# First transfers reordered and split, and twelve products of zeros ahead of the first real one, in a one-core encoder layer

## The chip, the cores and the metric

The kernel runs on one core of one Trainium2 chip. The core has a matrix engine (PE, with its own weight loads, PEld), a vector engine (DVE), a scalar engine (ACT), GpSimd (POOL), a queue engine (SP) that here starts the transfers, and 16 DMA engines that the queues share. The metric is the device time of one execution in microseconds (us); lower is better. It is given as the median of several runs.

## The reference: what is computed

One layer of an encoder trunk on x of 1 x 2048 x 1024 in float32. Cut to what matters here:

```python
xn = rms_norm(x, mix_norm_g)                 # mean of squares over 1024 features, then a gain
proj = xn @ w_in                             # w_in: 1024 x 5640
aq, ak, av, mq, mk, mv, mo, i, f, ga, gm = split(proj)
A = chunk_band_attention(aq, ak, av, rel_bias)     # 8 heads, own chunk of 64 and 8 before it
M = mlstm_chunkwise(conv(mq), conv(mk), mv, i, f)  # 4 heads, matrix memory
y = sigmoid(ga) * (A @ w_att_proj) + sigmoid(gm) * (M @ w_mlstm_proj)
x = x + y @ w_out
x = x + relu(rms_norm(x) @ w_up) ** 2 @ w_down
out = rms_norm(x)
```

The first thing that the matrix engine computes is `av`, the attention values of the first 512 tokens.

## The kernel before, in words

The 2048 tokens are worked in four blocks of 512. A float32 product is made of three products of a rounded form (fp32r): a value is split into a high part (a copy rounded to fp32r, on ACT) and a low part (the value less its high part, on DVE), and `mm3` (L642) multiplies high by high, high by low and low by high into one PSUM bank (lines 644, 645 and 646). Later parts of the program use seven instead of eight products of quarter matrices (`quad`, line 727).

Weights come as tiles of 128 x 1024 float32 (512 KB). `loader` (L509) starts their transfers into four raw tiles, `wraw`; `split_w` (L563) starts the transfer and `split_now` (L579) makes the two parts into one of three `wsp` tiles: ACT's copy is line 583, DVE's subtraction line 585. The first four weight tiles make `av` for the first block. Each of them covers two depth tiles of 128 features and 512 columns.

Block 0 is not normalised before its first products. `norm_in` and `square_in` (L1171) load x, transposed, as eight depth tiles of 128 x 512 (256 KB, line 1178), multiply each with its gain on ACT into the high part (line 1182), make the low part on DVE (line 1184), square it on ACT (line 1192) and add up the squares on DVE (line 1196); the rows are scaled by the root when a bank is emptied. The gains are in `gcol`, 12 KB, whose transfer is the second on SP (`setup`, line 430). Transfers of x and of the first four weight tiles take turns by events (`x_sent`, `w_sent`).

`token_tiles` (L666) multiplies: per weight tile, four token tiles `t` (one PSUM bank each), and in each two depth tiles `k`, three products each; 24 products for a weight tile, 96 for `av`. x is the stationary operand there, the weights move.

Two planners set the order. `Flow` runs the program's parts as threads with estimated times and gives out buffers and banks. `Order` then takes all instructions, their dependences and estimated durations, and writes a fixed order for each engine. PE's order goes by the thread's order among what is ready, the others' by due times. So the order on an engine is fixed before the run, and an instruction waits for the one ahead of it on its engine and for its operands.

Of the kernel before, what the change touches and what calls it, by code (L numbers as in the profile page):

```python
# [24 lines left out]
F32 = mybir.dt.float32  # L25
# [5 lines left out]
P = 128  # L31
# [4 lines left out]
NT = T // P  # L36
# [59 lines left out]
class Flow:  # L96
# [7 lines left out]
               act=dict(pe=220.0, act=130.0, dve=130.0, pool=180.0),  # L104
               dve=dict(pe=220.0, act=130.0, dve=130.0, pool=155.0), pool=dict(pe=290.0, act=130.0, dve=60.0),
               sp=dict())
# [106 lines left out]
def act_ns(n, ps=False, ap=0):  # L213
    return (51 if ps else 93) + 0.834 * n + 93 * ap


def dve_ns(n):
    return 70 + 1.042 * n
# [154 lines left out]
class Layer:  # L373
# [50 lines left out]

    def setup(self):
        nc, io = self.nc, self.io
        nc.vector.memset(self.half, -0.5)
        nc.vector.memset(self.ones, 1.0)
        yield "sp", 50
        nc.sync.dma_start(self.gcol, io["gcol"].rearrange("p (a b) -> p a b", a=3))  # L430
        self.fl.set(self.ev_gain)
        yield "wait", [self.w_sent[2]]
        yield "sp", 700, 2000
        nc.sync.dma_start(self.const, io["consts"].rearrange("p (a b) -> p a b", a=2))
        self.fl.set(self.ev_const)
# [73 lines left out]
    def loader(self):  # L509
        fl, io = self.fl, self.io  # L510
        i = 0
        for kind, n in self.weights():
            if kind == "quad":
                raws, evs = [], [Event() for _ in range(4)]
                fl.spawn(self.quad_w(i, *n, raws, evs), 0)
                for j in range(4):
                    (raw,) = yield "get", self.wraw, 1
                    raws.append(raw)
                    fl.spawn(self.load_w(io["wf"][n[0], j], raw, evs[j]), 0)
                i += 7  # L520
                continue
            first = kind == "plain" and i < KT // 2
            if kind == "plain":
                src = io["w"][n]
            else:
                q, m = n
                given, x = ((0, 0), (0, 2), (1, 0), (1, 1), (0, 3), (1, 2), (1, 3))[m]
                if given and q in self.td_ev:
                    yield "wait", self.td_ev[q]
                src = (io["wf"][q], self.td[q].ap() if given else None)[given][x]  # L530
            (raw,) = yield "get", self.wraw, 1
            if first:
                yield "wait", [self.x_sent[2 * i]]
            fl.spawn(self.split_w(i, src, raw, self.w_sent[i] if first else None), 0)
            i += 1

    def sum_w(self, q):
# [25 lines left out]
    def split_w(self, i, src, raw, sent=None):  # L563
        yield "sp", 1750, 2000
        self.nc.sync.dma_start(raw, src)
        if sent is not None:
            self.fl.set(sent)
        yield from self.split_now(i, raw)
        self.fl.put(self.wraw, raw, late=self.LATE)

    def slot_w(self, i):

        if i > 0:
            yield "wait", [self.wgot[i - 1]]
        (w,) = yield "get", self.wsplit, 1
        self.fl.set(self.wgot[i])
        return w
# [88 lines left out]
    def token_tiles(self, srcs, evs, after):  # L666

        fl = self.fl
        bank = [None] * NT
        nw = len(srcs) // 2  # L670
        for i in range(nw):
            w = yield from self.next_w()
            wv = w.rearrange("p a (k c) -> p a k c", k=2)
            for t in range(NT):
                if i == 0:
                    (bank[t],) = yield "dense", self.banks, 1
                for k in range(2):
                    g = 2 * i + k
                    if evs[g] is not None:
                        yield "wait", [evs[g]]  # L680
                    yield "pe", 681
                    a = srcs[g][:, :, t * P:(t + 1) * P]
                    self.mm3(bank[t], a[:, 0], a[:, 1], wv[:, 0, k], wv[:, 1, k],
                             g == 0, g == 2 * nw - 1)
                if i == nw - 1:
                    fl.spawn(after(t, bank[t]), 1)
            fl.put(self.wsplit, w, late=self.LATE_SPLIT)

# [1900 lines left out]
```

## Time and profile before

| | us |
|---|---|
| median of 3 runs | 2778.67 |
| lowest and highest of them | 2775.3 and 2782.26 |
| span of the profiled execution (first to last instruction) | 2771.8 |
| PE busy in it | 2749.0 |
| first product starts at | 6.37 |

For the profiled execution only its span is given, with no time of its own beside it; the median of the runs lies 6.87 us above that span. PE is busy for 99% of the span. "Busy" counts a product from its start to its end, and products overlap: one of 512 columns lasts about 0.39 us, and the next starts about 0.227 us after it. The distance between starts is therefore the rate. Times in the views are from the first instruction on. A transfer has a time of issue on its queue and, later, one of landing.

### The profile page before, as it was taken

To read this page: it belongs to the slowest core of one execution; us is meant where nothing else is said; L and a number is where in the kernel's file an instruction comes from. 1 tells how busy PE (TensorE), PEld (TensorE's weight loads), DVE (VectorE), ACT (ScalarE), POOL (GpSimd) and SP (SyncE) were. 2 spreads that over 40 slices of the span, in tenths; PEclk is the share of its full clock that TensorE was granted. 3 is DMA by queue.
4 is the path that set the end of the run, shared out by engine and by line. 5 is a ranking of instruction groups with operands and counts; after the bars stand their busy time and mean duration, and the time that the engine had idled before them with its cause. 6 is when DMAs were issued, how large, how long until landed. Compare 5 with 4: busy or idle time off the path is not lost.

```text
span 2771.8 us, 38590 instructions
## 1 busy us (share of the span) xinstructions
PE 2749.0 (99%) x12994; PEld 2285.1 (82%) x12994; DVE 2056.7 (74%) x3783; ACT 1491.5 (54%) x2608; POOL 54.7 (2%) x100
## 2 busy tenths in 40 slices
PE   9999999999999999999999999999999999999998
PEld 7888888888778888888888888888888888888887
DVE  7796789768996866886676688889888656555565
ACT  5564576535454535575555566666335655554443
POOL 0010001000000000000000000000000000000000
PEclk9999999999999999999999999999999999999999
DMA  7968759768765677589877977877977667766574
GB/s 275 294 193 276 230 166 306 248 224 318 258 205 203 220 252 255 194 273 326 289 280 273 296 236 233 257 228 234 290 247 254 209 220 262 242 239 218 190 229 151
DMA packets 329046, 678.64 MB, mean 245 GB/s; under 512 B 36840, under 2 KB 67728, under 8 KB 328848
## 3 DMA queue, kind: packets, MB, share of 16 engines
q1 hardware_dynamic: 328848, 676.18, 73.0%
q8 instruction: 102, 1.67, 0.3%
q14 instruction: 96, 0.79, 0.1%
HBM read 472.59 MB, written 203.44 MB: 244 GB/s over the span
## 4 chain that ended last, share of the span: by engine, by line
PE 94%; DMA 2%; DVE 2%; issue 2%; ACT 0%; SPq 0%; POOLq 0%; POOL 0%; DVEq 0%; ACTq 0%
PE bank L727 44%; PE bank L644 12%; PE bank L645 12%; PE bank L646 12%; PE bank L1417 2%; PE bank L1390 2%; PE bank L1448 2%; PE bank L755 2%; PE bank L1702 1%; PE bank L1703 1%; PE bank L1704 1%; PE bank L1688 0%; DVE wsp L585 0%; DMA r<-u 0%; DMA r<-kfar 0%
## 5 line engine op out<-in xcount | busy, mean ns | idle before, releaser
L727 PE MATMUL bank<-r,wsp 128*128 128x512 f32 x5544 | 1265.6, 390 | 0.9 <-DVE ctx L2083 0.4
L727 PEld LDWEIGHTS bank<-r,wsp 128*128 128x128 f32 x5544 | 1037.9, 188 | 222.3 <-DVE ctx L1869 3.7
L585 DVE TENSOR_TENSOR wsp<-wraw,wsp 128x1024 fp32r<-128x1024 f32 x459 | 561.2, 1223 | 357.6 <-ACT wsp L583 353.3
L583 ACT CAST wsp<-wraw 128x1024 fp32r<-128x1024 f32 x459 | 482.3, 1051 | 506.0 <-PE bank L727 210.6
L644 PE MATMUL bank<-r,wsp 128*128 128x512 f32 x1472 | 586.4, 399 | 1.8 <-ACT r L1226 1.6
L645 PE MATMUL bank<-r,wsp 128*128 128x512 f32 x1472 | 575.2, 391 | 0.2 <-DVE r L1231 0.2
L646 PE MATMUL bank<-r,wsp 128*128 128x512 f32 x1472 | 575.2, 391 | 0.0
L646 PEld LDWEIGHTS bank<-r,wsp 128*128 128x128 f32 x1472 | 276.4, 188 | 58.6
L644 PEld LDWEIGHTS bank<-r,wsp 128*128 128x128 f32 x1472 | 277.0, 188 | 54.1 <-ACT r L1226 1.8
L645 PEld LDWEIGHTS bank<-r,wsp 128*128 128x128 f32 x1472 | 277.2, 188 | 50.7 <-DVE r L1231 0.5
L1869 DVE TENSOR_TENSOR ctx<-bank,ctx 128x512 f32<-128x512 f32 x186 | 127.0, 687 | 89.4 <-PE bank L727 89.3
L1231 DVE TENSOR_TENSOR r<-r 128x512 fp32r<-128x512 f32 x248 | 164.5, 686 | 23.5 <-ACT r L1226 23.0
L1226 ACT CAST r<-r 128x512 fp32r<-128x512 f32 x248 | 149.1, 620 | 51.9 <-DMA r<-u 48.4
L1861 ACT COPY ctx<-bank 128x512 f32<-128x512 f32 x186 | 107.8, 581 | 65.7 <-PE bank L727 62.7
L1432 ACT ACTIVATE sc<-sc,scs 128x640 f32<-128x640 f32 (+4 forms) x128 | 97.4, 762 | 59.8 <-DVE scs L1429 53.8
L2200 ACT ACTIVATE ctx<-ctx 128x512 f32<-128x512 f32 x96 | 60.6, 631 | 103.9 <-DVE ctx L1869 103.9
L1453 DVE TENSOR_TENSOR r<-bank,r 128x512 fp32r<-128x512 f32 (+1 forms) x168 | 97.2, 597 | 18.9 <-ACT r L1451 18.2
L1423 DVE CUSTOM_DVE_ANT_0 sc<-bank,bias 128x320 f32<-128x320 f32 (+3 forms) x240 | 103.5, 462 | 6.4 <-PE bank L1417 4.3
L1451 ACT CAST r<-bank 128x512 fp32r<-128x512 f32 (+1 forms) x168 | 81.9, 518 | 35.6 <-PE bank L1448 28.2
L1390 PE MATMUL bank<-r,r 128*128 128x512 f32 x336 | 95.4, 365 | 2.0 <-DVE r L1453 1.8
L602 DVE TENSOR_TENSOR wraw<-wraw,wraw 128x1024 f32<-128x1024 f32 x76 | 92.9, 1223 | 2.1
L552 DVE TENSOR_TENSOR ctx<-ctx,ctx 128x512 f32<-128x512 f32 x112 | 76.5, 688 | 19.6 <-DMA ctx<-in_wf 12.9
(258 smaller groups left out, 2715.7 us busy)
## 6 DMA issues: line engine op xcount, KB each, us to landing
wraw<-in_wf SPq DMA_DIRECT2D x178, 512.0 KB, 4.4
wraw<-wsum SPq DMA_DIRECT2D x136, 512.0 KB, 4.7
r<-u SPq DMA_DIRECT2D x224, 256.0 KB, 4.3
wraw<-in_w SPq DMA_DIRECT2D x88, 512.0 KB, 5.2
u<-ctx SPq DMA_DIRECT2D x128, 256.0 KB, 2.2
ctx<-in_wf SPq DMA_DIRECT2D x112, 256.0 KB, 4.7
wsum<-ctx SPq DMA_DIRECT2D x112, 256.0 KB, 3.3
u<-tmp SPq DMA_DIRECT2D x96, 256.0 KB, 3.9
```

The costliest lines, as they stand in the source:

```text
L583: nc.scalar.copy(w[:, 0], raw)
L585: nc.vector.tensor_sub(w[:, 1], raw, w[:, 0].bitcast(F32))
L644: mm(ps, lh, rh, start=first, stop=False)
L645: mm(ps, lh, rl, start=False, stop=False)
L646: mm(ps, ll, rh, start=False, stop=last)
L727: mm(ps, wv[:, x, k, n], a[:, y], start=new and k == 0 and x == y == 0, stop=k == 3 and x == 1, skip_group_check=True)
L1226: self.nc.scalar.copy(dst[:, 0], src)
L1231: self.nc.vector.tensor_sub(dst[:, 1], src, dst[:, 0].bitcast(F32))
L1390: nc.tensor.matmul(acc[:, :, c0:c0 + w], st, sl[:, :, o:o + w], start=n == 0, stop=n == total - 1)
L1423: nc.vector.tensor_tensor_reduce(out=e[:, x * w:x * w + w], in0=bks[x][:, :w], in1=br[:, j0 + x * w:j0 + x * w + w], op0=ALU.add, op1=ALU. ...
L1861: nc.scalar.copy(t[:, o:o + 512], ps)
L1869: nc.vector.tensor_add(t[:, o:o + 512], ps, t[:, o:o + 512])
```

## The change: what it does

There are four edits, all at the program's start.

- The order of the first transfers on SP is the first half of the first weight tile, the first depth tile of x, the second half, the second depth tile of x, and then as before. The halves are the tile's two depth tiles (columns 0 to 511 and 512 to 1023). Each half is split by its own ACT copy and DVE subtraction (`split_first`).
- The transfer of the gains is started from ACT's queue and not from SP's.
- For the first weight tile alone, `token_tiles` runs over depth outside and token tiles inside.
- At the start DVE writes zeros into `maskb` (128 x 128, bf16; its real content is written later, as before), and PE makes twelve products of 512 columns of these zeros into a bank that nobody reads. Then the bank goes back.

```diff
     def setup(self):
         nc, io = self.nc, self.io
+        nc.vector.memset(self.maskb, 0.0)
         nc.vector.memset(self.half, -0.5)
         nc.vector.memset(self.ones, 1.0)
+        (bk,) = yield "get", self.banks, 1
+        for _ in range(12):
+            nc.tensor.matmul(bk.rearrange("p (c t) -> p c t", c=NT), self.maskb[:, 0],
+                             self.maskb.to_broadcast([P, NT, P]), start=True, stop=True)
+        self.fl.put(self.banks, bk)
         yield "sp", 50
-        nc.sync.dma_start(self.gcol, io["gcol"].rearrange("p (a b) -> p a b", a=3))
+        nc.scalar.dma_start(self.gcol, io["gcol"].rearrange("p (a b) -> p a b", a=3))
         self.fl.set(self.ev_gain)
...
-            fl.spawn(self.split_w(i, src, raw, self.w_sent[i] if first else None), 0)
+            fl.spawn(self.split_first(src, raw) if i == 0 else
+                     self.split_w(i, src, raw, self.w_sent[i] if first else None), 0)
...
+    def split_first(self, src, raw):
+
+        fl, nc = self.fl, self.nc
+        w = yield from self.slot_w(0)
+        halves = [slice(0, 512), slice(512, 1024)]
+        for s in halves:
+            yield "sp", 900, 2000
+            nc.sync.dma_start(raw[:, s], src[:, s])
+        fl.set(self.w_sent[0])
+        for s in halves:
+            yield "act", act_ns(512)
+            nc.scalar.copy(w[:, 0, s], raw[:, s])
+            yield "dve", dve_ns(512)
+            nc.vector.tensor_sub(w[:, 1, s], raw[:, s], w[:, 0, s].bitcast(F32))
+        self.wtile[0] = w
+        fl.set(self.wev[0])
+        fl.put(self.wraw, raw, late=self.LATE)
...
             wv = w.rearrange("p a (k c) -> p a k c", k=2)
-            for t in range(NT):
-                if i == 0:
+            by_k = self.wi == 1
+            for x in range(2 * NT):
+                t, k = (x % NT, x // NT) if by_k else (x // 2, x % 2)
+                if i == k == 0:
                     (bank[t],) = yield "dense", self.banks, 1
-                for k in range(2):
-                    g = 2 * i + k
...
```

What this makes of the engines' orders is shown at two places. The first is SP, the program's first transfers; `wraw_64` is the first raw weight tile, `ctx_113` on are the depth tiles of x. Before:

```order
L565 DMA wraw_64<-in_w 128x1024
L430 DMA gcol<-in_gcol 128x24
L1178 DMA ctx_113<-in_xt 128x512
L1178 DMA ctx_114<-in_xt 128x512
L565 DMA wraw_65<-in_w 128x1024
L1178 DMA ctx_115<-in_xt 128x512
```

In the changed kernel:

```order
L585 DMA wraw_64<-in_w 128x512
L1204 DMA ctx_113<-in_xt 128x512
L585 DMA wraw_64<-in_w 128x512
L1204 DMA ctx_114<-in_xt 128x512
L572 DMA wraw_65<-in_w 128x1024
L1204 DMA ctx_115<-in_xt 128x512
```

The first depth tile of x stands behind 256 KB and not behind 524 KB; from the second depth tile of x on, the same bytes are ahead as before, less the gains, which now stand first on ACT.

The second place is DVE, from the first weight tile's low part on; `wsp_61` is the first split tile, `r_68`, `r_69`, `r_70` and `r_71` hold the high and low parts of the first four depth tiles of x, `ctx_112` the sum of squares. Before:

```order
L585 TENSOR_TENSOR wsp_61<-wraw_64,wsp_61 128x1024
L1184 SCALAR_TENSOR_TENSOR r_68<-ctx_113,gcol,r_68 128x512
L1196 TENSOR_TENSOR ctx_112<-ctx_112,tmp_108 128x512
L1184 SCALAR_TENSOR_TENSOR r_69<-ctx_114,gcol,r_69 128x512
L585 TENSOR_TENSOR wsp_62<-wraw_65,wsp_62 128x1024
L1196 TENSOR_TENSOR ctx_112<-ctx_112,tmp_109 128x512
L1184 SCALAR_TENSOR_TENSOR r_70<-ctx_115,gcol,r_70 128x512
L1184 SCALAR_TENSOR_TENSOR r_71<-ctx_116,gcol,r_71 128x512
```

In the changed kernel:

```order
L591 TENSOR_TENSOR wsp_61<-wraw_64,wsp_61 128x512
L1210 SCALAR_TENSOR_TENSOR r_68<-ctx_113,gcol,r_68 128x512
L591 TENSOR_TENSOR wsp_61<-wraw_64,wsp_61 128x512
L1222 TENSOR_TENSOR ctx_112<-ctx_112,tmp_108 128x512
L1210 SCALAR_TENSOR_TENSOR r_69<-ctx_114,gcol,r_69 128x512
L610 TENSOR_TENSOR wsp_62<-wraw_65,wsp_62 128x1024
L1222 TENSOR_TENSOR ctx_112<-ctx_112,tmp_109 128x512
L1210 SCALAR_TENSOR_TENSOR r_70<-ctx_115,gcol,r_70 128x512
L1210 SCALAR_TENSOR_TENSOR r_71<-ctx_116,gcol,r_71 128x512
```

The subtraction of 1024 columns became two of 512, the second behind the first x tile's low part; the rest stands as before. PE's twelve products stand ahead of its first real one; its first 24 real products run, before and now, through the first depth tile for all four token tiles ahead of most of the second's. Behind the program's start no order changes on any engine; the PSUM banks' names are rotated by one, one for one.

More of the change, by code (lines that the diff above doesn't have):

```diff
@@ L673, in token_tiles @@
             wv = w.rearrange("p a (k c) -> p a k c", k=2)
-            for t in range(NT):
-                if i == 0:
+            by_k = self.wi == 1
+            for x in range(2 * NT):
+                t, k = (x % NT, x // NT) if by_k else (x // 2, x % 2)
+                if i == k == 0:
                     (bank[t],) = yield "dense", self.banks, 1
-                for k in range(2):
-                    g = 2 * i + k
[L679 to L685, printed above, removed]
+                g = 2 * i + k
+                if evs[g] is not None:
+                    yield "wait", [evs[g]]
+                yield "pe", 681
+                a = srcs[g][:, :, t * P:(t + 1) * P]
+                self.mm3(bank[t], a[:, 0], a[:, 1], wv[:, 0, k], wv[:, 1, k],
+                         g == 0, g == 2 * nw - 1)
+                if g == 2 * nw - 1:
                     fl.spawn(after(t, bank[t]), 1)
```

## The prediction

> **What bounds the kernel now.** I read the page's first lines, then PE's waits, then the chain of waits at the start, then PE's, ACT's and DVE's timelines there, and the stages' windows last.
>
> ```profile
> span 2771.8 us, 38590 instructions
> PE 2749.0 (99%) x12994; PEld 2285.1 (82%) x12994; DVE 2056.7 (74%) x3783; ACT 1491.5 (54%) x2608; POOL 54.7 (2%) x100
> ...
> PE bank L644 <- ACT r L1182: 6.4, 1, 6.4
> PE bank L1390 <- DVE r L1453: 1.8, 1, 1.8
> PE bank L755 <- DVE ctx L1869: 1.7, 2, 1.3
> ```
>
> PE sets the time nearly everywhere. Of the 22.8 us in which it is idle, 6.4 are one wait: the first product's, for the high part of the first x tile. The change works on that wait and on what follows it at once. The chain of waits shows what the wait is made of (start, length, what):
>
> ```profile
> 0.73 0.39 SPq L565
> ...
> 1.17 0.42 SPq L430
> ...
> 1.64 3.86 DMA ctx<-in_xt
> ...
> 5.59 0.73 ACT r L1182
> ...
> 6.37 2.07 PE bank L644 x4
> ```
>
> The last thing to come is the first x tile: issued third on SP, behind 512 KB of weights and the gains, landed at 5.50; then 0.72 of ACT.
>
> ```profile
> 6.37 2.07 PE L644 MATMUL bank<-wsp,r 128*128 128x512 f32 x4 [6.37 <-ACT r L1182]
> 8.24 1.91 PE L645 MATMUL bank<-wsp,r 128*128 128x512 f32 x4
> 9.95 0.93 PE L646 MATMUL bank<-wsp,r 128*128 128x512 f32 x3
> 10.71 0.40 PE L644 MATMUL bank<-wsp,r 128*128 128x512 f32 x1
> 10.94 0.39 PE L645 MATMUL bank<-wsp,r 128*128 128x512 f32 x1
> ...
> 13.67 0.39 PE L644 MATMUL bank<-wsp,r 128*128 128x512 f32 x1
> ```
>
> PE's timeline shows a second loss. Four products from 8.24 to 9.95 start 0.428 us apart; from 10.71 on they start 0.227 apart. So the first 24 products (6.37 to 13.67) take 7.3 us, where 24 x 0.227 = 5.45 is the usual price. The profile's clock row says 1.00 there, but a later place shows the same signature with the clock recorded: after the 1.84 us wait that ends at 121.99, products last 0.63 instead of 0.39 and start 0.43 apart, and the stage's clock is 0.84.
>
> ```profile
> 121.99 0.74 PE L1390 MATMUL bank<-r,r 128*128 128x512 f32 x2 [1.84 <-DVE r L1453]
> ...
> 124.75 0.63 PE L644 MATMUL bank<-r,wsp 128*128 128x512 f32 x1
> 125.18 0.63 PE L645 MATMUL bank<-r,wsp 128*128 128x512 f32 x1
> ...
> 126.33 0.39 PE L645 MATMUL bank<-r,wsp 128*128 128x512 f32 x1
> ...
> 122.00:133.00 11.00, 11.00 (x53) 9.55 (x54) 9.45 (x31) 6.94 (x17) 0.58 (x4) 0.84 0.91 273
> ```
>
> A clock of 0.84 over 11 us is half speed for about 0.16 x 11 / 0.5 = 3.5 us. I read the start the same way: half speed from the first product at 6.37 until about 9.95, 3.58 us, and full speed after it.
>
> **The change part by part.** *First transfers.* The DMA engines are busy from 1.75 on:
>
> ```profile
> 1.75:4.12 2.37, 0.00 (x0) 0.00 (x0) 0.25 (x2) 0.26 (x1) 0.00 (x0) 1.00 1.00 290
> 4.12:5.59 1.47, 0.00 (x0) 0.00 (x0) 0.39 (x1) 1.04 (x1) 0.00 (x0) 1.00 0.99 300
> 5.59:6.37 0.78, 0.00 (x1) 0.00 (x1) 0.78 (x2) 0.78 (x2) 0.00 (x0) 1.00 1.04 383
> ```
>
> (the last number is GB/s, the one ahead of it the DMA share). The x tile now has 256 KB (262 kB) less ahead of it. At 290 to 300 GB/s that is 0.87 to 0.90 us, at 383 it is 0.68. The other end: if only the issue counted, x is issued 0.47 earlier (the gains' 0.42 and the gap) and lands at 5.03. So it lands between 4.60 and 5.03; I take 4.8, near 0.68, since smaller rows may move no faster. Half a weight tile lands well before that, and ACT's copy of it, 0.62 us by the 512-column row below, ends before x comes. The gains' transfer on ACT's queue costs ACT one issue (0.42 on SP), ahead of an idle wait of 2.12 us until 4.12, which hides it; without that cover it would cost 0.42. Then 0.72 on ACT and 0.06 to PE: operands are ready for the first real product at 5.6 (5.4 to 5.85).
>
> ```profile
> L1226 ACT CAST r<-r 128x512 fp32r<-128x512 f32 x248 | 149.1, 620 | 51.9 <-DMA r<-u 48.4
> L1231 DVE TENSOR_TENSOR r<-r 128x512 fp32r<-128x512 f32 x248 | 164.5, 686 | 23.5 <-ACT r L1226 23.0
> ...
> 4.12 1.04 ACT L583 CAST wsp<-wraw 128x1024 fp32r<-128x1024 f32 x1 [2.12 <-DMA wraw<-in_w]
> ```
>
> *Twelve products of zeros.* No bf16 product of 512 columns is in the trace; the fp32r product of the same columns is the nearest row. They wait for one DVE memset:
>
> ```profile
> 0.80 0.06 DVE L428 MEMSET ones<- 128x2 f32 x1 [0.80 <-PEq L2576]
> ```
>
> so PE starts at about 0.95. What the first one costs beyond the usual distance is 0.16 (the first four before take 1.87 to the next, less 4 x 0.428). If all run at half speed they end at 0.95 + 0.16 + 12 x 0.428 = 6.25; if at full speed, at 0.95 + 12 x 0.227 = 3.7. If full speed comes after 3.58 us, as it did before, eight run at half speed until 4.53 and four more end at 5.44. I take this. It is 0.16 before the operands are ready, so the first real product starts at 5.6 and at full speed; with all twelve at half speed it starts at 6.25.
>
> This rests on when the clock is released. [...]
>
> *The run through the first tiles.* At full speed the first 24 products save 7.3 - 5.45 = 1.85, and the earlier start 6.37 - 5.6 = 0.77, 2.62 in all, if the operands keep up. These are ACT's and DVE's rows that decide it:
>
> ```profile
> 7.35 0.61 ACT L1192 ACTIVATE tmp<-ctx 128x512 f32<-128x512 f32 x1
> 8.14 1.04 ACT L583 CAST wsp<-wraw 128x1024 fp32r<-128x1024 f32 x1 [0.18 <-DMA wraw<-in_w]
> ...
> 8.00 0.69 DVE L1196 TENSOR_TENSOR ctx<-ctx,tmp 128x512 f32<-128x512 f32 x1 [0.90 <-ACT tmp L1192]
> 8.61 0.75 DVE L1184 SCALAR_TENSOR_TENSOR r<-ctx,gcol,r 128x512 fp32r<-128x512 f32 x1
> ...
> 11.01 1.41 DVE L1184 SCALAR_TENSOR_TENSOR r<-ctx,gcol,r 128x512 fp32r<-128x512 f32 x2
> ```
>
> ACT's work up to the second square starts 0.7 earlier but has a copy of half a tile (0.62) in between, so DVE's addition at 8.00 and the low part of the second x tile (end 9.36) stay within 0.3 of where they are. PE wants that low part as the 16th product, at 5.6 + 15 x 0.227 = 9.0: a wait of 0.1 to 0.4. The second weight tile's copy at 8.14 waited for its transfer, and the bytes ahead of that one are the same as before. So from there ACT and DVE run as before, and the fourth x tile's low part is ready at 11.01 + 1.41 = 12.42. PE wants it as the 30th product, at 5.6 + 29 x 0.227 = 12.2, or a little later because of the first wait; it starts at about 12.45. Before, the 30th stood at 13.67 + 5 x 0.227 = 14.8. **The saving is 14.8 - 12.45 = 2.35 us**: of the 2.62, 0.27 go into a new wait for DVE. Behind that the operands lead by more than PE does. In the late case (start at 6.25, full speed) the 30th product is at 12.83 and the saving is 1.97.
>
> The order over depth tiles costs and saves nothing: PE's order ran through the first depth tile first already. The halved split adds one ACT instruction (2 x 0.62 - 1.04 = 0.2) and one on DVE (2 x 0.69 - 1.22 = 0.15), counted in the 0.3 above. The rest of the program keeps its order, so the shift goes to the end unless a wait on the way takes it back. The sum: 2771.8 - 2.35 = 2769.45 for the span. The median of the runs lies 6.87 above the profiled span; 2769.45 + 6.87 = **2776.3 us**, 0.08% below the median.
>
> **The rivals.** *The shift is taken back where the DMA engines are the bound.* From 50 to 120 us their share is full:
>
> ```profile
> 50.00:100.00 50.00, 50.00 (x240) 41.01 (x239) 31.92 (x85) 26.15 (x50) 0.00 (x0) 1.00 1.01 326
> 100.00:120.00 20.00, 19.95 (x111) 16.75 (x109) 15.52 (x56) 10.65 (x28) 0.58 (x4) 1.00 1.05 317
> ...
> 40.00:50.00 10.00, 10.00 (x46) 8.29 (x45) 9.55 (x29) 3.98 (x8) 0.00 (x0) 1.00 0.49 165
> ...
> 105.79 7.83 DMA r<-kfar
> 113.63 6.03 DMA mixa<-tmp
> ```
>
> The chain goes through two transfers there and ends in the 1.84 us wait at 121.99. If their end doesn't move, that wait grows to 4.2 and the time stays: 2778.7. Against it: from 40 to 50 the share is 0.49, so the full stretch begins with transfers that wait for PE's results, and begins earlier too.
>
> *The zeros don't raise the clock.* Then all twelve run at half speed, the first real product starts at 6.25, and the half-speed stretch follows as before: 0.12 saved, 2778.55. For it: nothing in the trace shows what the clock goes by. Against it: at 122 the clock followed PE's idleness.
>
> *Slower.* One mechanism: at 122, with the transfers unmoved as in the first rival, PE's wait of 4.2 us is long enough for a second stretch of 3.5 us at half speed. That stretch costs 3.5 x (1 - 0.227/0.43) = 1.65: 2780.3. It decides only if the wait there grows beyond about twice its 1.84.
>
> **How the numbers follow.** Forecast (2776.3): 0.57. Taken back: 0.19. Zeros without effect: 0.11. Slower by 1.65: 0.10. The rest, 0.03, is something that no view shows. About 0.3%, 8.3 us, is what a measurement of this kernel can tell from no change. The edited place holds no more than 6.4 + 1.85 = 8.2 us altogether, so faster by more needs luck in the runs: 0.05. Slower by more: 0.04. Within: 0.91. The three runs of before spread over 7 us, which is more than all cases differ. So the range takes the cases, 2776.3 to 2780.3, and about half of that spread below and a little above them: 2771.5 to 2781.5.
>
> **What would show it.** Right: the first real product at 5.4 to 6.3 and 0.227 from one start to the next within its first tile; a short new wait of PE for line 1210 near 9 or 12; the product that stood at 13.67 at about 11.3; PE's wait near 120 still below 2.5 us. Wrong: products 0.43 apart after the zeros (second rival); PE's first wait shorter but the one near 120 longer by the same (first); a second stretch of clock below 0.9 there (third); the x tile landing after 5.1, which would mean that neither bytes nor issue held it back.

## The result: faster by 0.16% in the first comparison

The changed kernel has a median of 2774.28 us (2771.25 to 2779.76, 13 executions) against 2778.67 for the kernel before (2774.19 to 2782.96, 13 executions). The ratio is 0.9984, 95% interval 0.9977 to 0.9992: 4.4 us faster, with 2.2 to 6.4 in the interval, and within the 0.3% that the prediction called no difference. The forecast was 2776.3, range 2771.5 to 2781.5. Two later executions, one of the kernel before at 7180.68 us and one with sixty zeros at 3959.94, fell in a slow state and are left out of every figure below.

The profiled execution of the change took 2772.18 us with a span of 2770.4. So 1.8 us lie around the span, not 6.87, and the profiled execution of before, with a span of 2771.8, was one of its quicker ones.

Here are the page's first lines of the change, then PE's longest waits. Lines 669 to 671 are now the three products, 432 the zeros, 1416 and 781 what was 1390 and 755.

```profile
span 2770.4 us, 38619 instructions
PE 2750.6 (99%) x13006; PEld 2284.9 (82%) x13006; DVE 2054.3 (74%) x3785; ACT 1492.5 (54%) x2609; POOL 53.8 (2%) x100
...
PE bank L1416 <- DVE r L1479: 3.2, 2, 2.4
PE bank L781 <- DVE ctx L1895: 2.1, 2, 1.7
...
PE bank L432 <- DVE ones L429: 1.0, 1, 1.0
```

The wait of 6.4 us for the first x tile is gone from the list; PE waits 1.0 us for its zeros. But the wait that was 1.84 us near 122 is now 3.2 us in two pieces. PE's and ACT's timelines at the start:

```profile
0.98 5.30 PE L432 MATMUL bank<-maskb 128*128 128x512 bf16 x12 [0.98 <-DVE ones L429]
5.72 0.99 PE L669 MATMUL bank<-wsp,r 128*128 128x512 f32 x1
6.50 0.62 PE L670 MATMUL bank<-wsp,r 128*128 128x512 f32 x1
6.93 0.42 PE L669 MATMUL bank<-wsp,r 128*128 128x512 f32 x1
7.19 0.40 PE L670 MATMUL bank<-wsp,r 128*128 128x512 f32 x1
...
11.99 0.39 PE L669 MATMUL bank<-wsp,r 128*128 128x512 f32 x1
...
3.85 0.62 ACT L589 CAST wsp<-wraw 128x512 fp32r<-128x512 f32 x1 [1.41 <-DMA wraw<-in_w]
4.56 0.72 ACT L1208 ACTIVATE r<-ctx,gcol 128x512 fp32r<-128x512 f32 x1
```

The zeros fill PE until 6.28, all at half speed (0.427 us from one start to the next). (The first real product is recorded from 5.72 on, since a product's record overlaps the one ahead of it.) The first x tile's high part is ready at 4.56 + 0.72 = 5.28, so the first real product stands behind the zeros and does not wait for data. Two real products still run at half speed; the record has the clock up at 6.98, and from there on the distance is 0.23. The 25th product stands at 11.99 and stood at 13.67: 1.68 us earlier. That shift holds unchanged until 108 us. From the 25th product on both kernels run the same products in the same order, so any of them can be compared; among the first 24 the order differs a little. The next row of each is the first one behind the gate products, before and now:

```profile
35.48 0.40 PE L644 MATMUL bank<-wsp,r 128*128 128x512 f32 x1
```

```profile
33.80 0.40 PE L669 MATMUL bank<-wsp,r 128*128 128x512 f32 x1
```

At 110 us the shift is gone. One product stands at 109.94 before, without a wait, and at 110.58 in the change, behind the longer of the two waits:

```profile
109.94 0.73 PE L1390 MATMUL bank<-r,r 128*128 128x512 f32 x2
```

```profile
110.58 0.73 PE L1416 MATMUL bank<-r,r 128*128 128x512 f32 x2 [2.37 <-DVE r L1479]
```

From there on the two profiles differ in ways that have little to do with the start, as the experiments show.

### The profile page after: what moved, and what is told of

It is laid out like the page before. It is cut to its first block, busy times and chain, and to the rows that moved or that the text cites. A ratio compares the mean times of both kernels' runs of the same rounds, so it can differ in the third digit from the quotient of the medians.

```text
span 2770.4 us, 38619 instructions
## 1 busy us (share of the span) xinstructions
PE 2750.6 (99%) x13006; PEld 2284.9 (82%) x13006; DVE 2054.3 (74%) x3785; ACT 1492.5 (54%) x2609; POOL 53.8 (2%) x100
## 4 chain that ended last, share of the span: by engine, by line
PE 89%; DMA 5%; DVE 3%; issue 2%; ACT 1%; SPq 0%; POOL 0%; POOLq 0%; DVEq 0%; ACTq 0%
PE bank L753 45%; PE bank L669 11%; PE bank L670 11%; PE bank L671 11%; PE bank L1443 2%; PE bank L1416 2%; PE bank L781 2%; PE bank L1474 2%; DMA r<-mfar 1%; DMA r<-u 1%; DVE wsp L610 1%; PE bank L1728 0%; PE bank L1729 0%; PE bank L1730 0%; PE bank L1714 0%
```

## The experiments

Theory A is that of the prediction: the saving at the start is carried to the end. Theory B: it is taken back where the DMA engines are full, and what the median gained comes from elsewhere. Theory C came later: the change saves more than its start. For every kernel the table gives the start of one and the same product less its start in the first profile of before, in us, at four places named by the time in that profile; each from one profiled execution. The last column is the mean time of its executions with the standard error (83 for before, 24 for the change, 22 for zeros alone, 11, 11 and 8 for the other three); the executions come from three series, and not every kernel was in each.

| kernel | 35.48 | 135.07 | 500.13 | 2700.08 | mean time |
|---|---|---|---|---|---|
| before | 0 | 0 | 0 | 0 | 2778.0 (0.3) |
| before, again | -0.23 | -0.86 | -0.53 | +1.42 | in the row above |
| change | -1.68 | -1.93 | -0.03 | -1.35 | 2775.2 (0.4) |
| change, again | -2.10 | -1.54 | -0.88 | +1.23 | in the row above |
| zeros alone | -1.50 | -1.97 | +0.22 | +6.13 | 2776.6 (0.6) |
| zeros alone, again | -1.65 | -1.63 | -0.46 | +2.57 | in the row above |
| transfers alone | -0.09 | +1.23 | +1.31 | +3.05 | 2778.5 (0.7) |
| ten zeros | -0.84 | -2.15 | -3.34 | +1.43 | 2774.8 (0.7) |
| sixty zeros | +8.58 | +6.91 | +9.02 | +10.66 | 2786.5 (1.1) |
| gains on SP | -1.20 | -2.49 | -1.47 | -0.27 | one execution, 2773.3 |

**The kernel before once more.** No edit.

> The kernel before, unchanged, run as if it were a change. Both theories expect a ratio of 1 within 0.1%, and its profile tells how far two executions of one program differ on their own. Theory A (the start's saving is carried to the end): products stand at the same times as in the first profile up to about 100 us, apart from the release of the clock at the start, which may differ by up to 1.6 us, and behind 100 us they keep that difference. Theory B (the saving at the start is taken back where the DMA engines are full, 100 to 120 us; what the median gained comes from stretches of half clock that fall elsewhere): whatever the difference at 50 us is, it is gone or replaced by another one at 135 us and at 500 us, by 1 to 3 us in either direction.

Ratio 1.0004 (0.9996 to 1.0013), as both theories expected. The two profiles of one program are 0.23 us apart at 35, and 1.4 us the other way round at 2700. So a difference of 1 or 2 us late in two profiles says nothing about an edit, while at 35 us the two differ less. PE's wait near 120 (waits from 100 to 130 us) is not the same either, 2.8 us in two pieces where it was 1.84 in one:

```profile
PE bank L1390 <- DVE r L1453: 2.8, 2, 1.8
```


**The transfers alone.** Taken out of the change:

```diff
-        nc.vector.memset(self.maskb, 0.0)
...
-        (bk,) = yield "get", self.banks, 1
-        for _ in range(12):
-            nc.tensor.matmul(bk.rearrange("p (c t) -> p c t", c=NT), self.maskb[:, 0],
-                             self.maskb.to_broadcast([P, NT, P]), start=True, stop=True)
-        self.fl.put(self.banks, bk)
```

> The change without the twelve products of zeros and their memset; transfers, halves, loop order and ACT's queue as in the change. [...] Theory A: a saving of 0.5 to 1 us of the change's 4.4, a median near 2778. Theory B: no difference, 2778.7, or as much as the change if the later waits decide.

Ratio 1.0005 (0.9996 to 1.0013): no gain seen. PE's timeline (lines 663 to 665 are the three products):

```profile
5.57 0.79 PE L663 MATMUL bank<-wsp,r 128*128 128x512 f32 x1 [5.57 <-ACT r L1202]
6.16 0.63 PE L664 MATMUL bank<-wsp,r 128*128 128x512 f32 x1
...
9.14 1.86 PE L665 MATMUL bank<-wsp,r 128*128 128x512 f32 x4
10.84 0.39 PE L663 MATMUL bank<-wsp,r 128*128 128x512 f32 x1
11.07 0.40 PE L664 MATMUL bank<-wsp,r 128*128 128x512 f32 x1
...
35.38 0.40 PE L663 MATMUL bank<-wsp,r 128*128 128x512 f32 x1
```

The first product does come 0.80 us earlier (5.57, not 6.37). But half speed then lasts until about 10.8, for 5.2 us and not 3.7, and the shift is down to 0.09. So in this execution the earlier start was spent on more products at half speed. As the length of half speed varies from execution to execution (6.0 and 4.4 us in the two profiles of the change, last section), this one profile does not show that an earlier start is worth nothing; the mean, 0.5 us above that of before with a standard error of 0.8, shows no gain either.

**The zeros alone.** Added to the kernel before; the transfers stay as they were:

```diff
+        nc.vector.memset(self.maskb, 0.0)
...
+        (bk,) = yield "get", self.banks, 1
+        for _ in range(12):
+            nc.tensor.matmul(bk.rearrange("p (c t) -> p c t", c=NT), self.maskb[:, 0],
+                             self.maskb.to_broadcast([P, NT, P]), start=True, stop=True)
+        self.fl.put(self.banks, bk)
```

> The kernel before with the memset and the twelve products of zeros alone; transfers as before. [...] Theory A: the saving is that of the half clock, 1.0 to 2.5 us, a median near 2776.5. Theory B: nothing of it reaches the end, 2778.7 within 1 us.

Ratio 0.9996 (0.9987 to 1.0005). In the trace (line 650 is the first of the three products):

```profile
0.98 5.19 PE L432 MATMUL bank<-maskb 128*128 128x512 bf16 x12 [0.98 <-DVE ones L429]
6.38 1.21 PE L650 MATMUL bank<-wsp,r 128*128 128x512 f32 x4 [0.20 <-ACT r L1188]
7.42 0.85 PE L651 MATMUL bank<-wsp,r 128*128 128x512 f32 x3
...
33.98 0.40 PE L650 MATMUL bank<-wsp,r 128*128 128x512 f32 x1
```

The first real product stands where it stood before (6.38), and from it on all run at full speed: 1.50 of the change's 1.68 us. So in this run the products of zeros brought the clock up, 5.0 us after the first of them. At 2700 the execution was 6.1 us late, by waits and stretches of half clock near 970 and 1550 us; the time alone would have hidden all of this. Two stages of the same profile (length, busy times, then the clock, the last number but two):

```profile
950.00:1000.00 50.00, 46.90 (x195) 38.25 (x194) 39.24 (x51) 21.79 (x32) 0.00 (x0) 0.93 0.91 326
1530.00:1570.00 40.00, 38.03 (x183) 31.55 (x183) 23.46 (x53) 15.42 (x32) 2.08 (x1) 0.96 1.00 346
```


**Sixty zeros.** In the change:

```diff
-        for _ in range(12):
+        for _ in range(60):
```

> The change with sixty products of zeros for twelve. They end at about 16.4 (16 at half clock until 6.9, the others 0.216 apart), so real products start some 10 us later than in the change and run without any wait for operands: at 36 us they are 9.9 us behind the change. Theory A: the delay is carried to the end one for one, median 2774.3 + 9.9 = 2784. Theory B: the stretch at 100 to 120 us is bound by transfers that do not wait for PE, so at 135 us no more than about 3 of the 9.9 us are left, median at most 2777.5.

Ratio 1.0032 (1.0022 to 1.0042), the mean 11.3 us above the change's, with a standard error of 1.2.

```profile
0.98 15.94 PE L432 MATMUL bank<-maskb 128*128 128x512 bf16 x60 [0.98 <-DVE ones L429]
16.57 0.58 PE L669 MATMUL bank<-wsp,r 128*128 128x512 f32 x1
...
44.05 0.40 PE L669 MATMUL bank<-wsp,r 128*128 128x512 f32 x1
...
PE bank L1416 <- DVE r L1479: 1.8, 2, 1.4
```

A delay of 10.3 us against the change at the first mark (44.05 less 33.80) is 12.0 at the last by that profile and 9.4 by the change's second one. So a delay of the start reaches the end, about one for one, and theory B falls for delays. For a saving this shows less: in the change the wait at 110 us swallowed 2 us of saving, and 8 of 10 us of delay are still passed on here. And some is swallowed here: at 135 us the delay against the change's two profiles is 8.8 and 8.5, some 1.4 to 2.2 us less than at the first mark, since PE's two waits, now at 119 and 130 us, are 1.8 us together (the last row, waits from 100 to 145 us) where the change has 3.2. At the end that loss is not seen any more.

**The change once more, and the zeros alone once more.** Two kernels as above, run together.

> The change itself once more, on another chip than the first time. Theory A (the saving of the start, 1.5 to 2.5 us by the traces, is carried to the end and scatter is added to it): a ratio near 0.9992, 2.3 us, and not 0.9984 again. Theory C (the change saves more than its start, since the waits and half-clock stretches further on become fewer): 0.9984 again, 4.4 us.

> The kernel before with the memset and the twelve zeros alone, once more, beside the change. Theory A: the zeros are nearly all of the change (their trace had 1.50 us of its 1.68 at 36 us), a ratio near 0.9994, within 1 us of the change in the same job. Theory C: clearly behind the change, by 2 us or more.

Ratios 0.9989 (0.9980 to 0.9998) and 0.9993 (0.9985 to 1.0002). The first interval holds the 0.9992 of theory A and the 0.9984 of theory C, so this series alone decides nothing. Over all executions the change saves 2.8 us with a standard error of 0.5, against 1.68 and 2.10 at the first mark (against before in its own two series it is 3.2, with 0.6): nearer to A than to C's 4.4, but about 1 us above the marks. The zeros alone save 1.4 (0.6). That the change beats them by 1.4 (in this series by 1.2, between what A and C expected) has a standard error of 0.7, while the traces' first mark shows about 0.3. The mean granted clock of the executions, 0.9981 for the change and 0.9980 before, allows C a few tenths of a microsecond from fewer stretches of half clock. Whether the transfers bring more than the mark shows is left open.

The release varies within one program. PE's rows of the change's second profile:

```profile
0.98 4.94 PE L432 MATMUL bank<-maskb 128*128 128x512 bf16 x12 [0.98 <-DVE ones L429]
5.57 0.58 PE L669 MATMUL bank<-wsp,r 128*128 128x512 f32 x1
5.99 0.39 PE L670 MATMUL bank<-wsp,r 128*128 128x512 f32 x1
6.21 0.39 PE L669 MATMUL bank<-wsp,r 128*128 128x512 f32 x1
...
100.00:115.00 15.00, 12.33 (x62) 10.56 (x62) 10.51 (x39) 7.20 (x19) 0.29 (x2) 0.89 1.07 301
```

Here the clock came up at about 5.4, the zeros ended at 5.9 and no real product ran at half speed: 2.10 us saved. The last row is the stage from 100 to 115 us, with its clock at 0.89: in this execution a stretch of half clock fell there.

**Ten zeros.** `range(10)` for `range(12)` in the change.

> The change with ten products of zeros for twelve. In the change's trace the zeros were in the way: operands were ready at 5.33, the zeros ran at half clock until 6.1. Ten end at 5.2 to 5.4. Theory A: the first real product starts at 5.3 to 5.5, two products earlier by place in the queue, and the mark that stands at 33.80 in the change comes up to 0.45 us earlier where the clock is released at the same time; in the median no more than 0.5 us, which 5 rounds can't tell. Theory C: nothing to be seen at the mark, the median may go anywhere within 4 us.

Ratio 0.9987 (0.9979 to 0.9996), not to be told from the change. The first real product did come at 5.51, but the mark at 35 is 0.84 later than in the change, not 0.45 earlier. The mean is 3.2 us (standard error 0.8) below that of before, where this profile's mark has only 0.84. So either the marks of other executions lie better, or something beyond the start helps; no run here tells which. PE's waits up to 14 us and rows of ACT's timeline:

```profile
PE bank L671 <- DVE r L1210: 0.9, 1, 0.9
PE bank L669 <- ACT r L1208: 0.4, 2, 0.3
...
6.02 0.62 ACT L589 CAST wsp<-wraw 128x512 fp32r<-128x512 f32 x1
7.90 0.72 ACT L1208 ACTIVATE r<-ctx,gcol 128x512 fp32r<-128x512 f32 x1 [1.26 <-DMA ctx<-in_xt]
```

Another limit shows: the second x tile was taken up 1.2 us later in this execution than in the change (7.90 against 6.67 on ACT), although its transfer was issued at the same time, 2.11. PE then waited for that tile's high part and, 0.95 us, for its low part on DVE.

**The gains back on SP.** In the change:

```diff
-        nc.scalar.dma_start(self.gcol, io["gcol"].rearrange("p (a b) -> p a b", a=3))
+        nc.sync.dma_start(self.gcol, io["gcol"].rearrange("p (a b) -> p a b", a=3))
```

> The change with the gains' transfer back on SP, second there as before, so that the halves and x stand behind it. If the issue on SP counts, the first x tile's copy on ACT starts 0.47 later than in the change (4.56), at 5.0; if the bytes ahead of it count, 0.1 later at most, at 4.6 to 4.7. The first real product starts with the zeros' end, 6.1 to 6.3, in both cases.

```profile
0.98 4.05 PE L432 MATMUL bank<-maskb 128*128 128x512 bf16 x12 [0.98 <-DVE ones L429]
5.44 0.50 PE L669 MATMUL bank<-wsp,r 128*128 128x512 f32 x1 [0.41 <-ACT r L1208]
...
4.67 0.72 ACT L1208 ACTIVATE r<-ctx,gcol 128x512 fp32r<-128x512 f32 x1 [0.52 <-DMA ctx<-in_xt]
...
1.18 0.42 SPq L436 DMA_DIRECT2D gcol<-in_gcol  x1
1.65 0.42 SPq L1204 DMA_DIRECT2D ctx<-in_xt  x1
```

The x tile, issued 0.48 later (1.65), was used 0.11 later (4.67 against 4.56): the later issue does not show, as expected where the bytes ahead decide. Whether the gains' move to ACT's queue brings the 0.11 is not shown, since with the gains on ACT's queue that tile was used at 4.51, 4.56 and 4.74 in three executions. The part of the expectation on the zeros missed: they ended at 5.0, since the clock came up earlier here than in any other profile (2.65 us after the first zero), and PE then waited 0.41 us for data.

## Why the prediction was right, and where its sizes were off

- **That the time stays within 0.3% and falls a little**: right. But the range held the prices of all rivals too, so lying in it says little for the mechanism. That the start saves 1.5 to 2.1 us is shown by the marks of the change and of the zeros alone. That as much arrives at the end is shown by the mean times alone, 2.8 (0.5) and 1.4 (0.6): in the traces it is gone at 110 us, there again at 135 and lost in the scatter by 2700.
- **First transfers.** The x tile was forecast to land at 4.8 (4.60 to 5.03); ACT took it at 4.56 in the change, 4.51 in its second profile and 4.74 with ten zeros. In the first two that is below the whole range, and ACT came straight from its copy, so the tile may have landed earlier still: the tile came 0.94 us or more earlier than before. The sum had 0.87 to 0.90 for half a weight tile at the stage's rate; the gains' 12 KB, which are no longer ahead either, add 0.04 at that rate. Operands were ready at 5.28, not at 5.6.
- **Twelve products of zeros.** The step "If full speed comes after 3.58 us ... I take this" failed in size. In the change full speed came 6.0 us after the first zero, so the case that I had priced with a start at 6.25 is the one that happened: the zeros ended at 6.28. Two real products still ran at half speed, so 1.68 was saved, and not the 1.97 of that case with full speed or the 2.35 of the forecast. The second profile, with release after 4.4 us, saved 2.10. The step took the 3.58 of one profile as the price. The ten profiles have from 2.65 (with the gains on SP) to 6.0 us after PE's first product, so 3.58 was one draw, and no run shows what sets the time.
- **The new wait for DVE**, 0.27 us: not in the change, since PE came later than assumed. It was there where the zeros ended earlier, and larger: 0.9 us with ten zeros and with the gains on SP, because ACT took the second x tile up about a microsecond later there (7.90 and 7.56, not 6.67).
- **The profiled execution and the median.** "The median of the runs lies 6.87 above the profiled span" mixed two things: 1.8 us around the span, and 5 us by which that execution was quicker than the median. As the saving was subtracted from both, the forecast was not hurt by it.
- **The signs.** The first product and its rate came as listed. The product that stood at 13.67 came at 11.99, not at about 11.3, and PE's waits near 120 are 3.2 us, not below 2.5.
- **Rivals.** *Taken back at 100 to 120*: at 110 us this is what the traces show. The product that stands at 109.94 before starts between 109.65 and 110.75 in every kernel but the sixty zeros, whether its start had saved 2.1 us or nothing; what had been saved is spent in a wait there. By 135 us the kernels with zeros are ahead again, by 1.5 to 2.5 us of the first profile of before and by 0.7 to 1.6 of its second, and some of that is half clock that the first profile of before had at 122. At 500 four of the six lie within 0.4 us of the two profiles of before. The prediction had said that "the shift goes to the end unless a wait on the way takes it back" and counted on none. In the traces a wait does take it back at 110, and how the mean times come to be lower all the same stays open. *Zeros without effect*: refuted by the zeros alone. *A second stretch of half clock*: it occurs, at 111 or 112 us in both profiles of the zeros alone and in the change's second (clock 0.89, 0.90 and 0.89 from 100 to 115 us), after waits of 1.8 to 2.7 us and not only beyond twice 1.84. But the kernel before has one as well, at 122 in its first profile (0.89 from 115 to 130).

## What to carry to other kernels

A busy share of 99% does not mean that a saving at the start runs through: a later wait for transfers can take it up, as at 110 us here, and only many executions tell what is left at the end. With half clock at the start, try zeros on an idle PE first: they gave 1.5 and 1.65 us at the first mark in two profiles, where transfers 0.8 us earlier gave 0.1 in one. To see effects of 0.1% in a kernel whose executions scatter by 2.6 us, compare the place of one and the same product early in the trace, and repeat the profile of the kernel before to learn where two executions of one program already differ.

## What was not expected of the hardware

The clock's release came at very different times after PE's first product: by the traces' records of the clock 3.7 and 3.6 us in the two profiles of before, 5.2 with the transfers alone, 6.0 and 4.4 in the change, 5.0 and 5.3 with zeros alone, 5.8 with sixty, 3.9 with ten, and 2.65 with the gains on SP. (That record begins with its first change, so that the views read 1.00 before the release.) Whether twelve zeros took 2.65 or 6.0 us to bring the clock up was luck as far as these runs go: the change alone has 6.0 and 4.4 in two executions, and both profiles of before happened to be near the quick end. What sets the time is not shown by any run.

Nor did every wait of PE bring the clock down. Two stretches of the first profile of before, then a stage of its second and one of the change (the clock is the last number but two):

```profile
115.00:130.00 15.00, 13.16 (x63) 10.96 (x62) 10.67 (x36) 8.15 (x21) 0.58 (x4) 0.89 0.98 301
122.73:126.14 3.41, 3.41 (x14) 3.02 (x14) 2.96 (x17) 1.62 (x6) 0.19 (x2) 0.50 1.04 271
```

```profile
115.00:130.00 15.00, 13.24 (x70) 10.99 (x69) 11.79 (x40) 8.96 (x21) 0.59 (x4) 1.00 1.01 316
```

```profile
100.00:115.00 15.00, 12.63 (x73) 10.73 (x72) 10.88 (x42) 7.57 (x20) 0.29 (x2) 1.00 1.07 296
```

In the first profile of before, after the wait of 1.84 that ends at 121.99, the clock is at half from 122.73 to 126.14. In its second profile PE was idle for 1.76 us of the same stage, and the clock stayed at 1.00. In the change a wait of 2.37, which ends at 110.58, halved nothing either. So the length of a wait alone did not decide in these three; what else did is not shown.
